# Another order of the memory places in three of the scan's rings

## The chip, the cores and the metric

The kernel runs on one core of one Trainium2 chip. The metric is the device time of one execution in microseconds; three runs are shown for the kernel before.

## The reference, cut to what matters

The program is a two-layer backbone over 256 context tokens and 1024 latent tokens, width 1024, 16 heads of 64. What bears on this change is the first layer: an RWKV mixer, which projects its tokens, runs a recurrent scan in two directions over the result and reads it out.

```python
k = xk @ lp['wk']
v = xv @ lp['wv']
def step(s, inp):
    w_t, k_t, v_t, a_t, b_t = inp[:5]
    sa = jnp.einsum('bhvk,bhk->bhv', s, a_t)
    s = s * w_t[:, :, None, :] + sa[..., None] * b_t[:, :, None, :] + v_t[..., None] * k_t[:, :, None, :]
    y = jnp.einsum('bhvk,bhk->bhv', s, inp[5])
    return s, y
s_fin, ys = lax.scan(step, s0, xs, reverse=reverse)
out = (yn + bonus) * st['g']
return out @ lp['wo']
```

Behind the mixer come a squared-ReLU MLP, a Fourier mixer and a second MLP.

## The kernel before, in words

The kernel runs through stages on one core: projections ("phase 1", 0 to about 632 us of the profile), the scan (to about 1226 us), the readout (to 1396 us), the first MLP, the Fourier mixer and the second MLP.

Phase 1 works through eight units, in the order r0, k0, r1, k1, v0, k2, v2, v1: one of the three big projections (r, k, v) over one of three column ranges (0 and 1 are the latent halves, 2 is the context). Their matmuls are on lines L621 (512 columns of tokens) and L624 (shorter forms). Beside each unit runs a low-rank part: L735 and L774 for decay and learning rate, with evictions on L793 and elementwise work on L800 to L809, and beside v1 the gate's low-rank part, whose second matmul is L578; its moving operand is a mixed token tile written by ACT (L431) and DVE (L463), and its result is evicted by L427 and L586. What the scan needs (R and a in `s_ar`, K and b in `s_bk`, v in `s_v`, the gate in `s_hg`) goes to DRAM scratch by DMAs of line L424 on SP's queue.

The scan takes 20 chunks of 64 tokens, four of them context, in two directions d = 0, 1 per step. A step loads its operands (L922, on SP's queue): a and R into a pair of tiles of ring L0/L1, K and b into ring bk, v into ring sv. Then come the scores: L957 on PE, evictions on DVE (L973, with the mask tile) and ACT (L966, L970); a triangular inverse that starts with the DVE transpose of line L1077; L1014 and L1023 bring v and the inverse into it; then the chain of states.

The readout turns y round (L1369, PE transposes), normalizes by head (DVE lines L1314 to L1328), adds and gates (L1389, L1391), splits the tile into a rounded part (L427) and the rest (L1276), and multiplies by wo: three matmuls (L368, L369, L370) for each product, "main matmuls" below. L1415 adds the result to the residual stream; L1442, L1447, L1449 and L1453 make the RMS norm of the MLP behind it, and L1472 and L1477 apply it. The 192 main matmuls of the last token range run from 1372 us to 1396 us.

On-chip memory is divided into places (U0 to U31, and X, S, W, M). Three tables name which rings lie in which places: FIRST_RINGS (tiles named a..), P1_RINGS (b..) and SCAN_RINGS (s..). A name such as sU_199 is a tile of the scan in a U place: sU_201 and 200 are U0 and U1, 199 and 198 are U2 and U3, 195 and 194 are U6 and U7, 189 is U12; bW_105 and sW_153 are both place W6, and bW_109 is W2. `slot(name)` hands out a ring's entries in turn. Two lines of `memory` make a ring entry of a later stage wait for all users that the same place had before:

```python
plan.follows.setdefault(k, []).extend(self.taken.get(p, ()))
self.taken[p] = self.taken.get(p, []) + keys
```

In phase 1 the places U2 and U3 hold moving tiles (ring x_) and U12 and U13 weights (ring w), both used to phase 1's last unit; U6 and U7 hold the context's tokens (ring hc), used by the context units k2 and v2; U14 holds latent tokens (hl). Place W6 is the last entry of ring pre, from which v1's results are stored, and later holds the scan's mask tile, loaded on L848.

A planner (class Plan) takes all operations with their dependences and costs. It starts the operation with the earliest planned start next, and among equals the one with the longest remaining tail, picks a PSUM bank or an engine where there is a choice, and so writes one program in order for each engine. PE also gets filler matmuls (L1851) where the plan sees it wait for a bank. On the chip every engine runs its program strictly in that order.

Of the kernel before, what the change touches and what calls it, by code (L numbers as in the profile page):

```python
# [18 lines left out]
P = 128  # L19
# [7 lines left out]
C = 64  # L27
# [53 lines left out]
class Plan:  # L81
# [194 lines left out]
_u = lambda *n: tuple((f"U{j}", 0) for j in n)  # L276
_halves = lambda *n: tuple((f"U{j}", at) for j in n for at in (0, 512))
SCAN_RINGS = (
    ("bk", (8, P), *_row(4, "X0", 0, 1024)), ("mab", (2, 16, 32), *_row(3, "X1", 0, 1024)), ("tr", (16, 32), ("X1", 3072)), ("vt", (8, 32), ("X1", 3584)),
    *[(f"L{h}", (8, P), *[(f"U{2 * j + h}", 0) for j in range(6)]) for h in range(2)],  # L280
    ("sv", (2, 8, C), *_u(12, 13, 14)), ("l2", (8, 2, C), *_u(15, 16, 17, 18, 19, 20)), ("bkt", (2, 8, C), *_u(21, 22, 23, 24, 25)),
    ("xd", (16, 32), ("U26", 0)), ("xt", (16, 32), ("U26", 512)), ("hp", (16, 32), ("U27", 0)), ("z", (16, 2, 16), ("U27", 512)),
    ("xs", (512,), ("S6", 0), ("W5", 0), ("W4", 0)), ("t", (8, C), ("U30", 0), ("U30", 512)), ("st", (8, C), ("U31", 0), ("U31", 512)),
    ("ta", (512,), ("S0", 0), ("S1", 0)), ("td", (16, 32), ("S2", 0), ("S3", 0)), ("x", (16, 16), ("S4", 0), ("S4", 256)),
# [1678 lines left out]
```

## Time and profile before

| | |
|---|---|
| median of three runs | 3021.74 us (3017.54 to 3023.11) |
| profiled execution, its own time | 3018.24 us |
| span of the profiled execution | 3016.5 us |
| mean granted clock of TensorE | 0.947 |
| PE busy | 2820.9 us (94%) |
| DVE busy | 1883.4 us (62%) |
| ACT busy | 997.1 us (33%) |

PE is TensorE's matmuls, DVE VectorE, ACT ScalarE, POOL GpSimd and SP the engine that issues most DMAs. "Busy" is a mean over all stages, which differ: a stage in which PE is full is bound by PE, and one in which no engine is full is bound by waits from one engine to another.

### The profile page before, as it was taken

The numbers are of one execution on the slowest core, as the hardware profiler recorded it, in microseconds if no ns is written. First come the engines' busy times: TensorE is split into PE (matmuls) and PEld (weight loads), VectorE is DVE, ScalarE is ACT, GpSimd is POOL, SyncE is SP. The second block draws the span as 40 slices with busy tenths as digits, with TensorE's granted clock in tenths as the row PEclk, the third lists the DMA queues.
The fourth block names the chain that finished last, engine by engine and source line by source line (L and its number), as shares of the span: only waits on it lengthen the run. The fifth ranks groups of instructions, "written<-read, shape, count | busy, mean of one in ns | idle before, by whom it ended". The sixth has DMA issues, their size and how long they took to land.

```text
span 3016.5 us, 63005 instructions
## 1 busy us (share of the span) xinstructions
PE 2820.9 (94%) x26640; PEld 2187.5 (73%) x26640; DVE 1883.4 (62%) x3380; ACT 997.1 (33%) x1971; POOL 496.4 (16%) x425
## 2 busy tenths in 40 slices
PE   9999989988878878899999999999899999999998
PEld 5443446467777767788788888887797888888887
DVE  5398685537777777787565565446876454454455
ACT  4264454445555655342212111212332111111111
POOL 2064353300000000120101011101421011011110
PEclk9999989978888888899999999999799999999999
DMA  9266475633444454622332232111211111111111
GB/s 283 84 167 187 133 194 169 183 98 100 131 137 135 139 151 131 216 95 84 99 108 88 87 109 91 53 57 34 86 40 48 49 57 47 38 56 50 39 42 57
DMA packets 297291, 312.88 MB, mean 104 GB/s; under 512 B 81024, under 2 KB 212224, under 8 KB 297008
## 3 DMA queue, kind: packets, MB, share of 16 engines
q1 hardware_dynamic: 295648, 304.01, 33.5%
q0 software_dynamic: 1360, 4.84, 0.5%
q8 instruction: 209, 3.42, 0.5%
q14 instruction: 74, 0.61, 0.1%
HBM read 246.38 MB, written 62.39 MB: 102 GB/s over the span
## 4 chain that ended last, share of the span: by engine, by line
PE 70%; DVE 11%; issue 4%; DMA 3%; ACT 3%; POOL 0%; SPq 0%; DVEq 0%; ACTq 0%; POOLq 0%
PE ps L368 17%; PE ps L370 17%; PE ps L369 17%; PE ps L621 4%; PE ps L624 3%; PE ps L957 2%; PE ps L1037 1%; PE ps L1059 1%; PE ps L1023 1%; DVE bU L460 1%; PE ps L1160 1%; PE ps L1014 1%; DVE rU L1276 1%; PE ps L1147 1%; DVE bS L803 1%
## 5 line engine op out<-in xcount | busy, mean ns | idle before, releaser
L368 PE MATMUL ps<-rU,rU 128*128 128x512 f32 (+3 forms) x2632 | 979.9, 372 | 13.6 <-DVE rX L1546 8.0
L370 PE MATMUL ps<-rU,rU 128*128 128x512 f32 (+3 forms) x2632 | 976.5, 371 | 8.0 <-DVE rU L1276 5.3
L369 PE MATMUL ps<-rU,rU 128*128 128x512 f32 (+3 forms) x2632 | 975.4, 371 | 0.1
L368 PEld LDWEIGHTS ps<-rU,rU 128*128 128x128 f32 x2632 | 501.9, 191 | 107.5 <-DVE rX L1546 8.8
L370 PEld LDWEIGHTS ps<-rU,rU 128*128 128x128 f32 x2632 | 501.9, 191 | 99.8 <-DVE rU L1276 6.9
L369 PEld LDWEIGHTS ps<-rU,rU 128*128 128x128 f32 x2632 | 502.3, 191 | 90.1 <-DVE rU L1360 0.4
L1546 DVE SCALAR_TENSOR_TENSOR rX<-ps,mods,rX 128x512 f32<-128x512 f32 (+1 forms) x528 | 375.8, 730 | 123.6 <-PE ps L370 121.7
L1525 ACT ACTIVATE rS<-ps 128x512 f32<-128x512 f32 x122 | 73.1, 599 | 679.2 <-PE ps L370 678.5
L1276 POOL TENSOR_TENSOR rU<-rW,rU 128x512 fp32r<-128x512 f32 x74 | 118.7, 1609 | 1004.2 <-PE ps L370 519.1
L624 PE MATMUL ps<-bU,bU 128*128 128x512 f32 (+1 forms) x544 | 238.5, 575 | 1.2 <-ACT bX L427 0.9
L427 ACT CAST rU<-rW 128x512 fp32r<-128x512 f32 x161 | 97.2, 616 | 351.9 <-PE ps L370 255.6
L427 DVE CAST rU<-rW 128x512 fp32r<-128x512 f32 x115 | 55.2, 490 | 215.9 <-PE ps L369 210.0
L1276 DVE TENSOR_TENSOR rU<-rW,rU 128x512 fp32r<-128x512 f32 x200 | 173.2, 884 | 24.0 <-ACT rU L427 23.6
L427 DVE CAST rU<-rS 128x512 fp32r<-128x512 f32 (+1 forms) x97 | 45.0, 469 | 226.2 <-ACT rS L1528 198.9
L624 PEld LDWEIGHTS ps<-bU,bU 128*128 128x128 f32 x544 | 100.5, 193 | 107.5 <-issue 98.0
L621 PE MATMUL ps<-bU,bU 128*128 128x512 f32 x304 | 142.3, 609 | 0.0
L957 PE MATMUL ps<-sU,sX 64*128 64x128 f32 (+1 forms) x1280 | 121.9, 337 | 18.4 <-DVE sU L973 5.7
L957 PEld LDWEIGHTS ps<-sU,sX 64*128 64x128 f32 x1280 | 108.3, 240 | 28.0 <-issue 8.2
L427 ACT COPY sU<-ps 32x512 f32<-32x512 f32 (+2 forms) x186 | 96.0, 517 | 75.6 <-PE ps L1160 33.0
L1276 POOL TENSOR_TENSOR rU<-rS,rU 128x512 fp32r<-128x512 f32 x42 | 65.4, 1559 | 294.4 <-ACT rU L427 133.7
L621 PEld LDWEIGHTS ps<-bU,bU 128*128 128x128 f32 x304 | 56.5, 192 | 61.2 <-issue 57.6
L973 DVE TENSOR_TENSOR sU<-ps,sW 64x256 f32<-64x256 f32 x160 | 67.5, 422 | 50.1 <-ACT sX L966 20.4
(275 smaller groups left out, 3693.0 us busy)
## 6 DMA issues: line engine op xcount, KB each, us to landing
rW<-in_mlp_w_dram SPq DMA_DIRECT2D x256, 256.0 KB
rW<-in_k_mwt_dram SPq DMA_DIRECT2D x96, 256.0 KB
sX<-s_bk SPq DMA_DIRECT2D x40, 512.0 KB
s_ar<-bU SPq DMA_DIRECT2D x32, 512.0 KB
sU<-s_ar SPq DMA_DIRECT2D x64, 256.0 KB
sW<-in_k_mwt_dram SPq DMA_DIRECT2D x64, 256.0 KB
bU<-in_rk_wk_dram SPq DMA_DIRECT2D x48, 256.0 KB
bU<-in_rk_wv_dram SPq DMA_DIRECT2D x48, 256.0 KB
```

The lines of the kernel that those rows point to most:

```text
L368: nc.tensor.matmul(out, w[0], x[0], start=start, stop=False)
L369: nc.tensor.matmul(out, w[0], x[1], start=False, stop=False)
L370: nc.tensor.matmul(out, w[1], x[0], start=False, stop=stop)
L427: self.nc.scalar.copy(out, src) if e == "act" else self.engines[e].tensor_copy(out, src)
L460: return self.plan.flex(durs, lambda e: self.engines[e].tensor_tensor(out, a, b, op), r, w)
L621: fn = lambda B=B, x=x, w=w, ms=ms, kt=kt: nc.tensor.matmul(B.tile, x[:, ms], w, start=kt == 0, stop=kt == KT - 1)
L624: fn = lambda B=B, x=x, w=w, ms=ms, kt=kt, n=n: nc.tensor.matmul(B.tile[:, :n], w[:, ms], x[:, :n], start=kt == 0, stop=kt == KT - 1)
L957: nc.tensor.matmul(BB[hh].tile[:, j * P : j * P + nr], bk[HR[hh], q, :], L[hh][HR[hh], q, :nr], start=True, stop=True)
L973: plan.add("dve", 0.41, lambda bv=bv, ro=ro, hh=hh, q4=q4, d=d, L=L: nc.vector.tensor_tensor(L[hh][ro, q4, 0:C], bv()[ro, :, 0:C], self.ma ...
L1276: plan.flex({"dve": n / 960 + 0.07, "pool": n / 440 + 0.08}, lambda e: self.engines[e].tensor_tensor(out(1), src(), f32(out(0)), ALU.subtr ...
L1525: plan.flex({"act": 0.53, "dve": 0.6}, lambda e, B=B, s=s: nc.scalar.activation(s.tile[:, :512], B.tile, AF.Relu) if e == "act" else nc.ve ...
L1546: plan.add("dve", n / 960 + 0.12, lambda B=B, m=m, n=n, xs=xs: nc.vector.scalar_tensor_tensor(xs(), B.tile[:, :n], self.mod(layer, 5, m), ...
```

## The change

The rings of the scan keep their places and their sizes. Only the order in which they are handed out is another: for a and R the pairs of places U0/1, 2/3, 4/5, 6/7, 8/9, 10/11 become U0/1, 6/7, 8/9, 10/11, 2/3, 4/5; for v U12, 13, 14 becomes U14, 12, 13; and for the transposed b and K (ring bkt) U21 to U25 becomes U23, 24, 25, 21, 22. The waits for a place's earlier users move with the place. (The change's title names moving tiles too; they are the earlier users of U2 and U3, and P1_RINGS is untouched.)

```diff
-    *[(f"L{h}", (8, P), *[(f"U{2 * j + h}", 0) for j in range(6)]) for h in range(2)],
-    ("sv", (2, 8, C), *_u(12, 13, 14)), ("l2", (8, 2, C), *_u(15, 16, 17, 18, 19, 20)), ("bkt", (2, 8, C), *_u(21, 22, 23, 24, 25)),
+    *[(f"L{h}", (8, P), *[(f"U{2 * j + h}", 0) for j in (0, 3, 4, 5, 1, 2)]) for h in range(2)],
+    ("sv", (2, 8, C), *_u(14, 12, 13)), ("l2", (8, 2, C), *_u(15, 16, 17, 18, 19, 20)), ("bkt", (2, 8, C), *_u(23, 24, 25, 21, 22)),
```

The planner works with other waits, and so writes other programs. PE's first 571 rows (to about 497 us) are the same, and so are its last 7333 (from the last main matmuls of the readout on, 1372 us), apart from buffer numbers; what lies between is in another order. Three places are shown.

PE at the end of phase 1, before, around the last L774, which is the low-rank matmul of unit k2 (bU_, bS_ and bW_ are tiles of phase 1, aU_98 is the gate's weight, ps_ PSUM banks):

```order
L621 MATMUL ps_92<-bU_137,bU_148 128x512
L621 MATMUL ps_90<-bU_137,bU_148 128x512
L774 MATMUL ps_94<-bU_129,bS_116 128x256
L774 MATMUL ps_95<-bU_129,bS_116 128x256
L774 MATMUL ps_97<-bU_129,bS_115 128x256
L774 MATMUL ps_96<-bU_129,bS_115 128x256
L735 MATMUL ps_94<-bF_206,bF_204 128x256
L578 MATMUL ps_95<-bW_109,aU_98 128x512
L578 MATMUL ps_94<-bW_105,aU_98 128x512
L578 MATMUL ps_95<-bS_114,aU_98 128x512
L578 MATMUL ps_94<-bS_113,aU_98 128x512
L578 MATMUL ps_95<-bW_111,aU_98 128x512
```

The same place in the program of the change:

```order
L774 MATMUL ps_97<-bU_129,bS_116 128x256
L774 MATMUL ps_96<-bU_129,bS_116 128x256
L578 MATMUL ps_94<-bS_114,aU_98 128x512
L578 MATMUL ps_95<-bS_113,aU_98 128x512
L621 MATMUL ps_93<-bU_123,bU_131 128x512
L735 MATMUL ps_97<-bF_206,bF_204 128x256
L621 MATMUL ps_92<-bU_123,bU_131 128x512
L621 MATMUL ps_90<-bU_123,bU_131 128x512
L621 MATMUL ps_91<-bU_138,bU_130 128x512
L578 MATMUL ps_94<-bW_111,aU_98 128x512
L578 MATMUL ps_95<-bW_110,aU_98 128x512
L621 MATMUL ps_93<-bU_138,bU_130 128x512
```

Before, the four last L774 are rows 698 to 701 of PE's program, and fifteen L578 follow in one block (rows 703 to 717). In the change the last L774 is row 685, and eight of the L578 stand in pairs between L621; a block of seven is left at rows 711 to 717. Both programs then go on with L621 at row 718.

SP's queue at the handover to the scan, before (s_v<-bW_105 stores the last result of v1 from place W6; sU_199 and 198 are the a and R tiles of step 0, direction 1; sW_153 is the mask in place W6):

```order
L424 DMA s_hg<-bW_111 128x512
L424 DMA s_v<-bW_111 256x1x256
L922 DMA sU_199<-s_ar_213 64x8x64
L922 DMA sU_198<-s_ar_213 64x8x64
L424 DMA s_v<-bW_105 256x1x256
L922 DMA sU_189<-s_v 64x512 x2
L848 DMA sW_153<-in_k_mask_dram 128x512
```

And in the change, where step 0, direction 1 has its tiles in sU_195 and 194, loaded earlier in the queue:

```order
L424 DMA s_v<-bW_105 256x1x256
L848 DMA sW_153<-in_k_mask_dram 128x512
L424 DMA s_v<-bW_110 256x1x256
L424 DMA s_v<-bS_114 256x1x256
L424 DMA s_hg<-bW_111 128x512
L424 DMA s_v<-bW_111 256x1x256
L922 DMA sU_199<-s_ar_210 64x8x64
L922 DMA sU_198<-s_ar_210 64x8x64
L922 DMA sU_189<-s_v 64x512 x2
L424 DMA s_v<-bW_109 256x1x256
```

The mask's load moved from behind the last store of v1 to behind one of the earlier ones: v1's result in place W6 is now finished before those in W2 and W0. On PE, eight of step 0's 64-column score matmuls (L957, rows of the program) stood among v1's last L621 before; now sixteen do, and the sixteen of direction 1 follow directly.

PE near the end of the readout, before (rU, rS are tiles of the readout, ones_79 and spot_80 constants of the norm): the last L1442 and what follows it.

```order
L1442 MATMUL ps5_94<-rS5_13071,ones_79 32x128 x4
L1442 MATMUL ps5_94<-rS3_13046,ones_79 32x128 x4
L368 MATMUL ps7_96<-rU14_13912,rU28_13291 128x256
L369 MATMUL ps7_96<-rU14_13912,rU28_13291 128x256
L370 MATMUL ps7_96<-rU14_13912,rU28_13291 128x256
```

In the change (L1851 is a filler):

```order
L370 MATMUL ps4_93<-rU17_13748,rU29_13431 128x256
L1442 MATMUL ps2_91<-rS0_13030,ones_79 32x128 x4
L1442 MATMUL ps2_91<-rS6_13201,ones_79 32x128 x4
L1851 MATMUL ps1_90<-ident_63 128x128 x7
L1453 MATMUL ps1_90<-rS1_13128,spot_80 128x128 x4
L1851 MATMUL ps5_94<-ident_63 128x128 x28
L1369 MATMUL ps5_94<-ident_63,rS1_13128 128x128
```

Between the last L1442 and the last range's block of main matmuls stood 192 main matmuls before (24, 72, 24, 30, 24 and 18, with transposes between them, rows 3966 to 4190). Now 24 stand there (12 and 12), with 72 fillers, and 216 main matmuls stand in one block ahead of the last L1442 (rows 3918 to 4133). Before, there were 13 fillers at this place.

## Rows read from the trace of the kernel before

**Rows 1.** The page: the span, and busy time of three engines with its share of the span and the number of instructions.

```profile
span 3016.5 us, 63005 instructions
PE 2820.9 (94%) x26640; PEld 2187.5 (73%) x26640; DVE 1883.4 (62%) x3380; ACT 997.1 (33%) x1971; POOL 496.4 (16%) x425
```

**Rows 2.** Busy time by stretch of the span: its two ends and its length, then busy us of PE, PEld (weight loads), DVE, ACT and POOL, the granted clock of PE, the DMA share and GB/s.

```profile
497.00:580.00 83.00, 82.66 (x260) 41.45 (x261) 51.07 (x89) 37.91 (x92) 34.06 (x40) 1.00 0.65 178
580.00:600.00 20.00, 15.43 (x34) 6.04 (x31) 14.54 (x21) 7.92 (x17) 11.75 (x15) 0.83 0.70 157
630.00:640.00 10.00, 4.00 (x29) 2.73 (x28) 1.54 (x4) 1.87 (x5) 1.04 (x2) 0.79 0.44 132
640.00:670.00 30.00, 28.45 (x407) 26.52 (x408) 20.91 (x57) 18.57 (x48) 1.82 (x2) 0.50 0.30 89
700.00:1226.00 526.00, 420.71 (x14022) 386.97 (x14024) 386.61 (x954) 297.36 (x657) 13.48 (x24) 0.84 0.45 134
1226.00:1300.00 74.00, 61.53 (x587) 58.98 (x584) 61.07 (x101) 27.62 (x56) 19.52 (x15) 0.93 0.65 210
1300.00:1330.00 30.00, 28.75 (x266) 27.69 (x265) 29.96 (x52) 13.84 (x28) 5.55 (x4) 1.00 0.39 124
1330.00:1350.00 20.00, 20.00 (x191) 19.34 (x190) 12.07 (x16) 5.09 (x8) 5.63 (x4) 1.00 0.11 35
1350.00:1372.00 22.00, 19.05 (x141) 18.63 (x140) 19.47 (x34) 11.90 (x20) 5.48 (x4) 0.84 0.32 102
1372.00:1396.00 24.00, 24.00 (x207) 24.00 (x206) 13.05 (x32) 2.62 (x5) 0.00 (x0) 1.00 0.45 143
```

**Rows 3.** PE in order of time at the end of phase 1 and the start of the scan: start, length of the row (of all its instructions together), line, count, and in brackets how long PE had been idle before it and who ended that.

```profile
565.38 14.00 PE L621 MATMUL ps<-bU,bU 128*128 128x512 f32 x32
579.31 1.13 PE L774 MATMUL ps<-bU,bS 64*128 64x256 f32 x8
...
582.75 1.88 PE L578 MATMUL ps<-bS,aU 128*128 128x512 f32 x4
...
587.37 2.12 PE L578 MATMUL ps<-bW,aU 128*128 128x512 f32 x4 [1.02 <-DVE bW L463]
592.92 3.78 PE L578 MATMUL ps<-bS,aU 128*128 128x512 f32 x4 [3.42 <-DVE bS L463]
596.49 4.48 PE L578 MATMUL ps<-bW,aU 128*128 128x512 f32 x8
...
625.11 6.28 PE L621 MATMUL ps<-bU,bU 128*128 128x512 f32 x14
...
638.85 4.12 PE L957 MATMUL ps<-sU,sX 64*128 64x64 f32 x32 [5.69 <-DVE sU L973]
```

**Rows 4.** DVE in order of time, with the same columns: the first step of k2's last elementwise work, the first masked eviction of the scan, and the first transpose of the inverse.

```profile
580.55 0.30 DVE L800 TENSOR_SCALAR bS<-bS 128x256 f32<-128x256 f32 x1 [8.02 <-ACT bS L793]
...
638.37 1.78 DVE L973 TENSOR_TENSOR sU<-ps,sW 64x256 f32<-64x256 f32 x4 [13.50 <-DMA sW<-in_k_mask_dram]
...
644.22 1.04 DVE L1077 STREAM_TRANSPOSE sS<-sX 128x512 f32<-128x512 f32 x1 [0.34 <-ACT sX L970]
```

**Rows 5.** SP's queue in order of time: start of issue, its length, and the DMA.

```profile
572.01 1.92 SPq L424 DMA_DIRECT2D s_bk<-bU  x3
...
585.04 2.14 SPq L424 DMA_DIRECT2D s_bk<-bU  x3
...
590.42 1.93 SPq L424 DMA_DIRECT2D s_bk<-bU  x3
...
632.75 0.58 SPq L424 DMA_DIRECT2D s_v<-bW  x1
633.38 1.25 SPq L922 DMA_DIRECT2D sU<-s_v  x2
635.43 0.34 SPq L848 DMA_DIRECT2D sW<-in_k_mask_dram  x1
```

**Rows 6.** PE in order of time in the readout: a long row of fillers, the last L1442, the L1453 behind it, the last transposes and fillers, and the first main matmul of the last range.

```profile
1249.00 8.65 PE L1851 MATMUL ps<-ident 128*128 128x128 f32 x76
...
1336.86 0.64 PE L1442 MATMUL ps<-rS,ones 128*32 128x128 f32 x16
...
1366.35 2.35 PE L1369 MATMUL ps<-ident,rS 128*128 128x128 f32 x20
...
1370.65 3.06 PE L1851 MATMUL ps<-ident 128*128 128x128 f32 x26
1373.47 0.37 PE L368 MATMUL ps<-rU,rU 128*128 128x256 f32 x1
```

**Rows 7.** DVE in order of time over the same stretch, from the norm's reciprocal to the splits that the last range's matmuls read.

```profile
1338.03 0.95 DVE L1449 RECIPROCAL rS<-rS 128x128 f32<-128x128 f32 x1 [0.58 <-ACT rS L1447]
1340.58 0.48 DVE L1415 SCALAR_TENSOR_TENSOR rX<-ps,mods,rX 128x256 f32<-128x256 f32 x1 [1.60 <-PE ps L370]
1342.16 2.27 DVE L1472 SCALAR_TENSOR_TENSOR rS<-rX,gs,rS 128x512 f32<-128x512 f32 x3 [1.10 <-ACT rS L427]
...
1366.55 0.48 DVE L1415 SCALAR_TENSOR_TENSOR rX<-ps,mods,rX 128x256 f32<-128x256 f32 x1 [2.53 <-PE ps L370]
...
1371.75 1.89 DVE L1276 TENSOR_TENSOR rU<-rS,rU 128x512 fp32r<-128x512 f32 x3
```

## Prediction

> **What bounds the kernel now.** I read the page's totals first: PE is busy for 94% of the span [rows 1], so on the whole time is saved only where PE waits or runs slowly. The table by stretch says where that is. PE is full to 580 us, has holes from 580 to 600 and from 630 to 640, runs at a granted clock of 0.50 from 640 to 670, and is 80% busy in the scan (420.71 of 526), where DVE is 73% busy: there no engine is full, and waits from one engine to another set the pace [rows 2]. So a scan that starts earlier should end earlier by about as much. In the readout DVE is full from 1300 to 1330 and PE from 1330 to 1350; from 1372 PE is full [rows 2]. As all programs are the same from 1372 us on, the question is when PE gets to that point.
>
> Then I read PE in order of time. Behind the 32 L621 come the last L774 at 579.31; the L578 that follow wait 1.02 and 3.42 us for DVE's line L463 [rows 3]. DVE itself had stood idle for 8.02 us before 580.55, because the L774 came so late [rows 4]: k2's elementwise work then stands ahead of the L463 that the L578 need. At the scan's start PE waits 5.69 us before 638.85 [rows 3], for a bank that DVE's L973 has to empty. That L973 had waited for the mask [rows 4], and SP issues the mask's load at 635.43, last in a row of stores and loads that reaches back to 632.75 [rows 5].
>
> **The change part by part.** It adds and removes no arithmetic; loads, stores and products are the same. Work moves in three places.
>
> *1. The gate's low-rank block.* In the change the last L774 is ahead of sixteen L621 that it stood behind; 32 take 14.00 [rows 3], so it comes 7 us earlier, and somewhat more as k2's second half no longer alternates with v0. The L578 are spread, and the last seven come at about the same place as before. The waits of 1.02 and 3.42 us should go: 4.4 us. Behind them twelve L578 took 3.78 + 4.48 = 8.26 us, where four usually take 1.88 [rows 3], so 5.64: another 2.6 us of low clock (0.83 over the 20 us [rows 2]). Together 7.0 us. What is late next: the stores of K and b (s_bk) are single-buffered; three go out at a time, and the last triples were issued at 572.01, 585.04 and 590.42 [rows 5], 5.4 us apart when nothing else holds them. Two triples behind 572.01 at that spacing end at about 583, 7 to 8 us earlier than now, and no more than that. The L463 for the last L578 would come 7 to 8 us earlier, against a PE that is 7 us earlier: nothing is left over. Bounds of that back pressure: 0 and 3.4 (the larger wait stays); I take 1.
>
> *2. The handover.* The last L621 end at 631.4 (625.11 + 6.28 [rows 3]). The first L973 starts 7.0 us behind that, and the inverse's first transpose 12.8 us behind it, at 644.22 [rows 4]. In the change the mask is loaded behind the store of a result that is finished some twelve L621 and sixteen score rows earlier, about 6 us. From that store's issue to the mask's is now 635.43 - 632.75 = 2.7 us [rows 5], and from there to L973 2.9 us, so the mask lands at about the end of the last L621, perhaps 1 us later. Direction 1's a and R lie in U6 and U7, loaded long before, so its scores follow directly. From L973 to the transpose stay 5.85 us [rows 4]; the transpose then stands about 7 us behind the last L621, not 12.8. The gain is 5.7 us, the 5.69 that PE waits [rows 3]. Bounds: 0, if the mask's wait on SP, which now has stores of v queued behind it, holds up the evictions from W0 and W2 that free banks; 8, if all of the 12.8 but the 5.0 of two score-and-eviction rounds goes.
>
> *3. The clock after the handover.* From 640 to 670 PE is busy for 28.45 of 30 us at a granted clock of 0.50, half of its 2.4 GHz, after a stretch in which it was busy for 4.00 of 10 [rows 2]. With the wait gone the clock may stay up. DVE is busy for 20.91 us in those 30 and its work doesn't shrink, so the bounds are 0 and 9; I take 1.5, near 0, because the scan afterwards has room on PE (80%) and does not go faster for it [rows 2].
>
> The Trainium skill ("TensorE: Matmul & The Clock Gate", section "What's actually happening") says that the half rate is the default and that recent activity lifts it. The trace agrees as far as the fall goes: 4.00 of 10 us busy, then 0.50. By that rule alone all of the 30 us would run at the full clock, and the sum would be some 7 us lower than mine.
>
> *4. The end of the readout.* This speaks against the change. Before, the last L1442 of the norm is at 1336.86, and from there to the last range's first main matmul at 1373.47, 36.6 us, PE has 192 main matmuls to do [rows 6] while DVE runs the norm and the last readout units, from 1338.03 on [rows 7]. A main matmul costs 0.116 us (207 in 24.00 [rows 2]), so the cover is 22.3 us. In the change 168 of these 192 are done ahead of the last L1442, which therefore comes 168 x 0.116 = 19.5 us later, at about 1356.4 in the old time; only 2.8 us of cover is left. How long the rest now takes has two bounds. From PE's rows alone: 32 transposes (20 take 2.35), 24 main matmuls, 1 us of L1453 and L1442, and 72 fillers (13, recorded as 26, take 3.06 [rows 6], so 72 take 16.9) make 24.5 us, and the last range starts at 1380.9: 7.4 us later. From DVE's chain: its 36.6 us hold waits for main matmuls of 1.60, 1.10 and 2.53 us [rows 7], which go; 31.4 remain, and the last range starts at 1387.8: 14.3 later. (PE's own waits there are only 2.95 us now, 22.00 - 19.05 [rows 2]; so nearly all of it is new.) DVE, full from 1300 to 1330, gets room from having to do its part later, and five fillers fewer run early in the readout, 1.2 us. I take 10, between the bounds.
>
> Sum against the profiled execution's own 3018.24: -7.0 + 1 - 5.7 - 1.5 + 10 = -3.2, so **3015 us**. That execution lies 3.5 us below the median of the runs shown (3021.74); what counts as no change is 0.2%, 6 us.
>
> **The rivals.** *A, the readout costs little.* DVE works ahead, because it no longer shares its full 1300 to 1330 with so many gating steps, and PE reaches the last L1442 earlier by most of the 12.5 us that it is idle from 1226 to 1300 (74.00 - 61.53 [rows 2]). For it: that idle time exists. Against it: the 72 fillers take PE's time whatever DVE does. Loss 0 instead of 10: 3005.
>
> *B, the clock.* All of the half-clock stretch is won back, 9 us instead of 1.5, and the readout costs its 10: 3007.5. Against it: the inverse is a chain through DVE and ACT, which were busy 20.91 and 18.57 of the 30 us [rows 2].
>
> *C, slower.* One mechanism: behind the last L1442 the chain through ACT and DVE keeps its whole 36.6 us, because each step waits for the one before and not for PE. Then the last range comes the full 19.5 us later, and the sum is -13.2 + 19.5 = +6.3: 3024.5. It decides from a loss of 19.2 on. For it: few of DVE's rows in that stretch show a wait for PE [rows 7], and 36.6 us is what the chain takes today. Against it: 5.2 us of it are such waits.
>
> *D, the change does nothing at the handover.* If v1's other stores and loads of v, and not the mask, set the scan's start, 5.7 of the gain goes, and the clock's 1.5: 3022.
>
> **How the numbers follow.** My forecast has a chance of 0.42, with its own range of 3009 to 3020; A 0.22, B 0.08, C 0.18, D 0.10. The range over all must leave out no more than 2 in 10: from below A with a little of B on top, 3000, to a little above C, 3027. Faster by over 0.2% (below 3012) are A, B and a third of my own case, 0.43; slower (above 3024) most of C and a little of D, 0.20; the rest, 0.37, is within 0.2%.
>
> **What would show it.** Right: no wait of the L578 for L463 and four of them in about 1.9 us; the first L973 within 2 us of the last L621 and the first L1077 about 7 behind it, at some 631 instead of 644; a readout in which PE stands or runs fillers for about 20 us between the last L1442 and the last range's first main matmul, which comes at about 1370. Wrong: if that matmul comes before 1362, the readout's price was mine only (A, B); if after 1376, C or D holds; if the distance from the first L1077 to the readout's first transposes differs by over 4 us, a reordered scan has a price of its own, which this sum sets at nothing because both programs run the same steps with neither PE nor DVE full.

## The result, and the profile after

The changed kernel takes 3030.85 us (median of six runs, 3026.94 to 3041.48) against 3019.64 us for the kernel before in the same comparison: a ratio of 1.0047, 95% interval 1.0032 to 1.0062. It is slower by some 14 us (10 to 19); 3015 was predicted, in a range of 3000 to 3027. The profiled execution has a span of 3028.9 us, 12.4 us more than before [rows 1].

The start of the scan came as forecast and better. PE in order of time at the end of phase 1, in the change (columns as in [rows 3]):

```profile
565.23 0.70 PE L774 MATMUL ps<-bU,bS 64*128 64x256 f32 x4
...
587.08 1.88 PE L578 MATMUL ps<-bS,aU 128*128 128x512 f32 x4
588.79 3.60 PE L578 MATMUL ps<-bW,aU 128*128 128x512 f32 x8
...
622.06 1.98 PE L621 MATMUL ps<-bU,bU 128*128 128x512 f32 x4
623.98 2.00 PE L957 MATMUL ps<-sU,sX 64*128 64x64 f32 x32
```

No L578 waits any more, and twelve of them take 5.48 us, not 8.26. The last L621 ends at 624.04, not 631.39, and the scores of step 0 follow it without a gap. DVE and SP at the handover (as in [rows 4] and [rows 5]):

```profile
619.68 0.88 DVE L973 TENSOR_TENSOR sU<-ps,sW 64x256 f32<-64x256 f32 x2 [0.60 <-ACT sX L966]
...
628.33 1.05 DVE L1077 STREAM_TRANSPOSE sS<-sX 128x512 f32<-128x512 f32 x1 [1.02 <-ACT sX L970]
```

```profile
576.55 1.95 SPq L424 DMA_DIRECT2D s_bk<-bU  x3
...
581.21 1.98 SPq L424 DMA_DIRECT2D s_bk<-bU  x3
...
613.53 0.33 SPq L848 DMA_DIRECT2D sW<-in_k_mask_dram  x1
```

The mask's load is issued at 613.53 instead of 635.43, L973 no longer waits for it but for ACT, and the first transpose of the inverse stands at 628.33 instead of 644.22: 15.9 us won.

The scan then gives all of it back. The first L1023 of steps 0, 8, 16 and 19 (the matmuls that bring inverse and right side together) show its two ends and two places between, before:

```profile
683.84 1.97 PE L1023 MATMUL ps<-sS,sU 64*64 64x64 f32 x32
...
903.63 0.33 PE L1023 MATMUL ps<-sW,sU 64*64 64x64 f32 x2
...
1135.06 0.33 PE L1023 MATMUL ps<-sW,sU 64*64 64x64 f32 x2
...
1220.03 0.33 PE L1023 MATMUL ps<-sW,sU 64*64 64x64 f32 x2 [0.46 <-ACT sU L427]
```

and in the change:

```profile
668.33 1.97 PE L1023 MATMUL ps<-sS,sU 64*64 64x64 f32 x32
...
879.60 0.30 PE L1023 MATMUL ps<-sW,sU 64*64 64x64 f32 x2 [0.69 <-DVE sU L427]
...
1138.68 0.33 PE L1023 MATMUL ps<-sW,sU 64*64 64x64 f32 x2 [0.46 <-ACT sU L427]
...
1220.75 0.33 PE L1023 MATMUL ps<-sW,sU 64*64 64x64 f32 x2 [0.23 <-ACT sU L427]
```

From the first to the last are 536.2 us before and 552.4 in the change, "scan length" below. The lead is 15.5 us at step 0, 24.0 at step 8, and gone at step 16: steps 8 to 16 take 259 us instead of 231, while the steps ahead of them and behind them take 8.5 and 2.9 us less than before. The granted clock over the whole scan is 0.87 in the change and 0.84 before, so the clock is not what makes it longer.

The readout's end costs what its order let expect. PE, as in [rows 6], in the change:

```profile
1356.15 0.43 PE L1442 MATMUL ps<-rS,ones 128*32 128x128 f32 x8 [0.88 <-ACT rS L1435]
1356.51 1.83 PE L1851 MATMUL ps<-ident 128*128 128x128 f32 x14
...
1359.06 6.42 PE L1851 MATMUL ps<-ident 128*128 128x128 f32 x56
...
1372.05 7.03 PE L1851 MATMUL ps<-ident 128*128 128x128 f32 x46 [1.95 <-ACT rS L1385]
...
1383.05 3.29 PE L1851 MATMUL ps<-ident 128*128 128x128 f32 x28
1386.09 0.36 PE L368 MATMUL ps<-rU,rU 128*128 128x256 f32 x1
```

The last L1442 is 19.3 us later than before, PE runs 18.6 us of fillers behind it (7 + 28 + 23 + 14 of them, recorded as twice that), and the last range starts at 1386.09, 12.6 us later than before [rows 6]. Of these, 11.9 arise behind the scan: from the first L1023 of step 19 to the last range are 165.3 us now and were 153.4. From there both programs run alike, and the spans differ by 12.4 us.

### The profile page after: what moved, and what is told of

Same layout as the page of the kernel before. It is cut to its first block, busy times and chain, and to the rows that moved or that the text cites. A ratio compares the mean times of both kernels' runs of the same rounds, so it can differ in the third digit from the quotient of the medians.

```text
span 3028.9 us, 63221 instructions
## 1 busy us (share of the span) xinstructions
PE 2816.7 (93%) x26750; PEld 2183.0 (72%) x26750; DVE 1883.3 (62%) x3377; ACT 997.9 (33%) x1978; POOL 489.9 (16%) x421
## 4 chain that ended last, share of the span: by engine, by line
PE 70%; DVE 12%; issue 4%; ACT 4%; DMA 3%; POOL 0%; SPq 0%; DVEq 0%; ACTq 0%
PE ps L368 17%; PE ps L370 17%; PE ps L369 17%; PE ps L621 4%; PE ps L624 3%; PE ps L957 2%; PE ps L1037 1%; ACT sU L427 1%; PE ps L1023 1%; DVE sU L973 1%; DMA rW<-s_y 1%; PE ps L578 1%; PE ps L1160 1%; DVE rU L1276 1%; PE ps L1059 1%
## 5 line engine op out<-in xcount | busy, mean ns | idle before, releaser
L368 PE MATMUL ps<-rU,rU 128*128 128x512 f32 (+3 forms) x2632 | 978.9, 372 | 12.2 <-DVE rX L1546 8.0
L427 DVE CAST rU<-rS 128x512 fp32r<-128x512 f32 x98 | 46.5, 480 | 230.5 <-ACT rS L1528 203.2
L621 PE MATMUL ps<-bU,bU 128*128 128x512 f32 x304 | 142.3, 606 | 0.0
L957 PE MATMUL ps<-sU,sX 64*128 64x128 f32 (+1 forms) x1280 | 116.0, 329 | 15.7 <-issue 5.2
L957 PEld LDWEIGHTS ps<-sU,sX 64*128 64x128 f32 x1280 | 103.4, 233 | 23.7 <-issue 8.7
L437 POOL TENSOR_SCALAR sU<-sS,sS 128x256 f32<-128x256 f32 x23 | 11.1, 486 | 556.9 <-DVE sS L1110 510.1
L621 PEld LDWEIGHTS ps<-bU,bU 128*128 128x128 f32 x304 | 56.0, 192 | 61.1 <-issue 58.2
```

The source lines that it names most:

```text
L368: nc.tensor.matmul(out, w[0], x[0], start=start, stop=False)
L427: self.nc.scalar.copy(out, src) if e == "act" else self.engines[e].tensor_copy(out, src)
L621: fn = lambda B=B, x=x, w=w, ms=ms, kt=kt: nc.tensor.matmul(B.tile, x[:, ms], w, start=kt == 0, stop=kt == KT - 1)
L957: nc.tensor.matmul(BB[hh].tile[:, j * P : j * P + nr], bk[HR[hh], q, :], L[hh][HR[hh], q, :nr], start=True, stop=True)
```

## Experiments

**Four mixtures of the two orders.** The planner is replaced by a list: for each operation its number, engine, place and fillers, in the order in which the planner of one or the other kernel had put it. Handover, scan and readout can then have either kernel's order. Where a place of the list isn't free in the mixture, the one that has been free longest is taken.

```diff
     def emit(self):
-        (the planner's loop over what is ready)
+        for entry in zlib.decompress(base64.b85decode(SEQUENCE)).decode().split(";"):
+            i, e, fills, slots = entry.split(",")
+            op, e, fills = real[int(i)], ENGINE_NAMES[int(e)], int(fills)
+            ...
+            for _ in range(fills if blank else 0):
+                self.fill(blank.tile)
+            op["fn"](e) if "durs" in op else op["fn"]()
```

e1 has the changed handover, and scan and readout in the old order:

> Places as changed. The order of all operations is written out instead of planned: the changed kernel's order up to the end of scan step 2, the order of the kernel before from there on, scan and readout. Theory 1 (each stretch's order has its own price: handover -16 us, scan +16, readout +12.6, as the two traces put it): about 3003, 16 us (to 24, the lead at step 3) under the kernel before. Theory 2 (something later holds the scan's end whatever its start, so any lead is lost on the way): no gain at the readout's first transposes, 3015 to 3020. Theory 3 (the places themselves cost the scan time): like theory 2.

e2 has the changed handover, the old scan and the changed readout:

> Places as changed, the changed order up to the end of scan step 2, the old order for the rest of the scan, the changed order from the scan's end on. Theory 1: -16 to -24 + 12.6, so 3 to 11 us under the kernel before. Theory 2: +12.6, like the changed kernel, near 3031. Theory 3: like theory 2.

e3 has the old handover, and scan and readout in the changed order:

> Places as before, the old order up to the end of scan step 2, then the changed kernel's order for the scan and the readout. Theory 1: +16 (to 24) + 12.6, so 3048 to 3056, the slowest of all. Theory 2: +12.6 alone, near 3031, as with the changed kernel. Theory 3: +12.6 at most, as the places are the old ones.

e4 has the old handover and scan, and the changed readout:

> Places and order as before up to the scan's end, the changed kernel's order from there on (the last range's main matmuls ahead of the norm). All three theories of the scan: +12.6 us, near 3032; the last L1442 some 19 us later than in the kernel before and the last range's first main matmul 12.6 later. If it is under +5, the readout's loss came from how the scan ended and not from its own order.

| | handover, scan, readout | median us (3017.93 for before) | ratio, 95% | scan length |
|---|---|---|---|---|
| e1 | new, old, old | 3002.71 | 0.9943 (0.9924 to 0.9962) | 537.8 |
| e2 | new, old, new | 3022.31 | 1.0013 (1.0000 to 1.0027) | 533.7 |
| e3 | old, new, new | 3050.63 | 1.0111 (1.0091 to 1.0132) | 555.9 |
| e4 | old, old, new | 3036.25 | 1.0060 (1.0043 to 1.0076) | 534.4 |

The ends of e1's and of e3's scan, as above for the two kernels:

```profile
667.25 1.97 PE L1023 MATMUL ps<-sS,sU 64*64 64x64 f32 x32
...
1205.03 0.32 PE L1023 MATMUL ps<-sW,sU 64*64 64x64 f32 x2 [0.46 <-ACT sU L427]
```

```profile
683.85 1.97 PE L1023 MATMUL ps<-sS,sU 64*64 64x64 f32 x32
...
1239.77 0.33 PE L1023 MATMUL ps<-sW,sU 64*64 64x64 f32 x2
```

Started early or late, in old or new places, the old order of the scan takes 534 to 538 us and the changed one 552 to 556. So theories 2 and 3 fall: a scan that starts 16.6 us earlier does end 15.0 us earlier, if its own order stays (e1), and the new places cost nothing that can be seen in it. By ratio the handover is worth -17 us (e1; -23 to -11), the readout +18 (e4; 13 to 23), and the scan's order +15 (e3 less e4; some 8 either way). The sum, +16, is near the changed kernel's +14, and handover and readout together (e2, +4) miss theirs by 3; e2 had been expected under the kernel before. e1 is faster than both kernels.

How the loss divides between scan and readout is less sure than its sum, because the readout's price hangs on the scan in front of it. The last range's first main matmul in e3 and in e4:

```profile
1405.82 0.36 PE L368 MATMUL ps<-rU,rU 128*128 128x256 f32 x1
```

```profile
1393.08 0.36 PE L368 MATMUL ps<-rU,rU 128*128 128x256 f32 x1
```

From the first L1023 of step 19 to there are 166.0 us in e3, nearly the changed kernel's 165.3, but 172.1 in e4 and 178.9 in e2, whose scans have the old order; with the old readout it is 153.4 before and 150.9 in e1. So the changed readout costs 12 to 13 us behind the scan that it was planned with, and 18.7 and 25.5 behind the other (e2's profiled execution lies 6 us above its median). e4's 18 is that of a mixture and not the price in the changed kernel, and e3 less e4 makes the scan's part too small: by the scan lengths it is 16.2 in the change and 19.7 in e3.

**The two parts of the change, planned as ever.** e9 turns only the ring of a and R, e10 only those of v and of bkt:

```diff
-    *[... for j in range(6)]) for h in range(2)],
+    *[... for j in (0, 3, 4, 5, 1, 2)]) for h in range(2)],
```

> One part of the change alone, planned as ever: only the ring of a and R takes its places in the new order. SP's queue has the mask early, as in the changed kernel; the readout has the old order (192 main matmuls between the last L1442 and the last range, 13 fillers). Theory 1 (each stretch's order has its own price): handover -16 us and no readout loss; with a scan as long as the old one about 3003, with one as long as the changed one about 3019. The handover itself must show the first L1077 near 628.

```diff
-    ("sv", (2, 8, C), *_u(12, 13, 14)), ... ("bkt", (2, 8, C), *_u(21, 22, 23, 24, 25)),
+    ("sv", (2, 8, C), *_u(14, 12, 13)), ... ("bkt", (2, 8, C), *_u(23, 24, 25, 21, 22)),
```

> The other part alone: the rings of v and of the transposed b and K in the new order, a and R as before. Handover and readout stand in the old order on all engines but a few SP rows. All theories: within 0.2% of the kernel before, near 3018.

e9 takes 3006.81 us against 3015.15, a ratio of 0.9977 (0.9957 to 0.9996), in a comparison in which both kernels spread widely (2997 to 3018, and 3008 to 3031). That is 7 us (1 to 13), where some 15 had been expected with a scan as long as the old one. Its profile has the early handover (first L1077 at 629.93), a scan of 539.4 us and the old readout; the last range starts at 1358.93, 14.5 us earlier than before:

```profile
1356.11 3.06 PE L1851 MATMUL ps<-ident 128*128 128x128 f32 x26
1358.93 0.37 PE L368 MATMUL ps<-rU,rU 128*128 128x256 f32 x1
```

The order of its scan is neither the old nor the changed one, so 539.4 prices a third order.

e10 takes 3021.36, a ratio of 1.0022 (1.0011 to 1.0033), with the first L1077 at 647.08 and a scan of 539.1. That is 7 us slower than the kernel before, just over the 0.2% that was expected at most, though all engines but SP have the rows of the kernel before in the same order and SP has all but two; why is open. The new places of these two rings may cost a little, or a difference of this size comes from elsewhere.

So the early start comes with the ring of a and R, and neither part alone has the changed kernel's scan or readout. The rings of a and R and of v together, built but not run, give the changed kernel's order row for row on all engines: the ring bkt has no part in the order, and the two losses need the other two rings turned together.

**What in the changed order makes the scan long.** Its side work differs: between the L1023 of steps 8 and 16, the changed order puts 40 of the 64 products that make the modulation vectors (DVE, L898; 64 weight tiles of 256 KB, L897), the old order 27. Twelve kernels cut or double parts of that side work, or free it of a wait, with the order of all engines untouched. All but e13 and e14 get a wrong modulation by it.

```diff
-        self.plan.add("q", 0.8, lambda: nc.sync.dma_start(w(), src), ...)
+        z = 8 if isinstance(kw, tuple) and kw in self.full else 512; self.full.add(kw)
+        self.plan.add("q", 0.8, lambda: nc.sync.dma_start(w()[:, :z], src[:, :z]), ...)
```

> The kernel before, order untouched; of the 64 weight tiles that the scan loads on the side for the modulation vectors (line L897, 256 KB each) all but the first four loads are cut to 8 of 512 columns, so the modulation is wrong and 15 MB are not moved. Read beside the same cut in the changed kernel: scan length from the first L1023 of step 0 to the first of step 19, 536.2 us before and 552.4 us in the change, a difference of 16.2. Theory A (PE's instruction supply waits behind data loads, and the changed order bunches loads): both scans get shorter, the changed one by 10 us or more beyond this one, and PE's waits with no visible cause (60 us here, 78 in the change) fall in both. Theories B and C: both shorter by a like amount, the difference stays at 12 to 18.

> The changed kernel with the same cut of side loads. Theory A: scan 552.4 falls to under 535, the difference to the old order under 6 us. Theory B (the side products on DVE, L898, of which the changed order has 40 between steps 8 and 16 and the old one 27, hold DVE): difference stays at 12 to 18. Theory C (the interleave of the scan's own operations): stays too.

e7 and e8 cut the products too:

```diff
-            w(), w(), 1.0, self.silr, ALU.mult, ALU.mult,
+            w()[:, :n], w()[:, :n], 1.0, self.silr[:, :n], ALU.mult, ALU.mult,
```

> The kernel before with the side loads cut as above and the 64 side products on DVE (L898) cut from 512 to 8 columns, order untouched; the modulation is wrong. Theory B: the scan gets shorter, and the difference to the changed order with the same cut falls under 6 us. Theory C: difference 12 to 18.

> The changed kernel with the side loads and the side products cut. Theory B: its scan falls by 10 us more than that of the kernel before with the same cut. Theory C: the difference of 12 to 18 us is still there, so it lies in the order of the scan's own operations.

e11 and e12 leave the loads whole and let the products read a constant tile:

```diff
-            w(), w(), 1.0, self.silr, ALU.mult, ALU.mult,
+            self.silr, self.silr, 1.0, self.silr, ALU.mult, ALU.max,
```

> The changed kernel, order untouched and all side loads whole, but the scan's 64 side products on DVE (L898) read a constant tile instead of the loaded one, so DVE never waits for a load; the modulation is wrong. If the loads cost the scan time by holding DVE in its queue, the scan (552.4 us from the first L1023 to the last step's) falls to about 535, as with the loads cut. If it is the loads' traffic, which delays other transfers and what PE has to fetch, it stays above 545.

> The kernel before with the same cut of the wait, as a control: no wait of a product for its load was seen in its scan, so 533 to 537 us.

e13 and e14 issue each side load twice in a row (`[nc.sync.dma_start(w(), src) for _ in range(1 + isinstance(kw, tuple))]`), e15 and e16 are e7's cut of the products with whole loads, e17 and e18 are e6 with z = 64 and z = 256:

> The kernel before, order untouched, each of the scan's 64 side loads (L897) issued twice into the same tile, so 16.8 MB more move; the result is unchanged. If traffic of the side loads costs scan time in proportion, in the old order too (3 us for cutting 15 MB), the scan of 536.2 us gets 3 to 5 longer. If an order loses only where its loads meet something, it may lose up to 20. If traffic costs nothing, 533 to 539.

> The changed kernel with each side load issued twice. Traffic theory: cutting 15 MB took 18 us off its scan of 552.4, so 16.8 MB more add 10 to 20 (562 to 572). If the loss is the interleave of the scan's own operations and the fall with the loads cut was something else: 550 to 556.

> The changed kernel with all side loads whole, and the 64 side products on DVE cut from 512 to 8 columns (the modulation is wrong). Traffic theory: the scan stays at 548 or more. If DVE's extra products in steps 8 to 16 were the cause: about 535.

> The kernel before with the same cut of the products, loads whole. Control: between 522.9 (loads and products cut) and 536.2 (nothing cut); traffic theory: about 526, so a difference of over 20 us to the changed order.

> The changed kernel with all but the first four side loads cut to 64 of 512 columns (the modulation is wrong). If the side loads' traffic is what makes the changed scan long, 534 to 539 us, as with 8 columns (534.4). If that single look was an exception and the loss lies in the interleave of the scan's own operations, 545 or more.

> The same with 256 of 512 columns. Traffic theory: between, 541 to 547. Interleave theory: 548 to 556, like the whole loads.

Scan length in us, each from one profile, and the part from step 8 to step 16:

| side work | old order | changed order | difference | steps 8 to 16: old, changed, difference |
|---|---|---|---|---|
| whole | 536.2 | 552.4 | 16.2 | 231.4, 259.1, 27.7 |
| loads of 256 columns | | 541.2 (e18) | | 247.5 in the change |
| loads of 64 columns | | 541.2 (e17) | | 249.8 in the change |
| loads of 8 columns | 533.2 (e5) | 534.4 (e6) | 1.2 | 233.3, 248.7, 15.4 |
| loads twice | 621.2 (e13) | 639.2 (e14) | 18.0 | 269.0, 313.4, 44.4 |
| products short, loads whole | 531.8 (e16) | 543.9 (e15) | 12.1 | 233.6, 252.9, 19.3 |
| products and loads short | 522.9 (e7) | 534.7 (e8) | 11.8 | 230.0, 243.3, 13.3 |
| products don't wait for loads | 547.2 (e12) | 557.5 (e11) | 10.3 | 238.6, 261.7, 23.1 |

The old order's five uncut scans (the kernel before, e1, e2, e4, e10) lie between 533.7 and 539.1, so a single look is good to some 3 us. Four things follow.

The products' waits for their loads are not the cause: freed of them, the changed scan is not shorter (e11). The control missed its expectation by 10 and is longer as well, for a reason that stays open.

The doubled loads don't measure traffic. Both loads of a pair write one tile, and on SP's queue the second waits for the first; the queue's waits in e13's and in e14's scan (us in total, times, longest):

```profile
SPq L897 <- DMA sW<-in_k_mwt_dram: 286.2, 64, 9.2
```

```profile
SPq L897 <- DMA sW<-in_k_mwt_dram: 268.3, 64, 9.0
```

The scan's other loads stand behind these in the queue. Both orders lose alike, 85.0 and 86.8 us, where 3 to 5 (at most 20) and 10 to 20 had been expected, and the rate only rises from 132 to 141 and from 130 to 138 GB/s. So e13 and e14 show what a held queue costs.

The side work is a part of the changed order's loss. In steps 8 to 16, where that loss lies, cutting the loads takes 9 to 12 us off the changed scan (e6, e17, e18), cutting the products 6 (e15) and cutting both 16 (e8); the old one gains next to nothing there (231.4 whole, 230.0 to 233.6 cut). The loads' size matters little: e18 and e17 are alike though one moves four times the other's bytes, and e17 fell between the two lengths expected for it, as e15 did.

But it isn't all. With loads and products cut the changed order is still 11.8 us longer, and 13.3 in steps 8 to 16. The 1.2 of e5 and e6, which theory A asked for, doesn't fit that: e6 has the shortest steps 0 to 8 and 16 to 19 of all changed scans, and with one look at each it is open whether that is chance. What is left can only lie in how the scan's own operations are interleaved, by e7 and e8 some 12 of the 16 us; no run here takes it apart further.

One thing in which the two orders differ there can be read from the trace: PE's longest waits for nothing that the profile names. Busy time by stretch, in the change (columns as in [rows 2]):

```profile
859.00:864.30 5.30, 4.57 (x222) 4.08 (x218) 5.09 (x17) 3.50 (x8) 0.00 (x0) 1.00 1.04 231
864.30:869.40 5.10, 0.02 (x4) 0.02 (x4) 0.00 (x0) 1.22 (x2) 0.00 (x0) 0.82 1.02 244
...
931.30:936.50 5.20, 0.04 (x6) 0.01 (x2) 1.95 (x7) 0.00 (x0) 0.00 (x0) 0.61 0.88 229
```

PE stands for 5.1 us in the middle of a run of equal matmuls, and the profile shows no engine or transfer that it waits for ("issue"):

```profile
930.93 0.40 PE L1160 MATMUL ps<-sU,sU 32*32 32x32 f32 x25 [0.47 <-DVE sU L1152]
...
936.49 1.60 PE L1160 MATMUL ps<-sU,sU 32*32 32x32 f32 x103 [5.16 <-issue]
```

The trace has the transfers of kind "instruction" too, in this window one of 16 KB on queue q8 (packets, MB, share of the 16 engines):

```profile
q8 instruction: 1, 0.02, 1.3%
```

It lasts from 934.00 to 935.09, 1.4 us before PE goes on; in the wait that ends at 869.38 another ends at 867.90, 1.5 us before. Such transfers come some 130 times in the scan, every 4 us or so, and all 21 "issue" waits of PE over 1.5 us in the change, and all 15 in the kernel before, end 1.3 to 1.7 us after one of them does. So by their timing PE waits there for its instructions. The side loads don't make these waits: with loads and products cut, in e8, the same one stands behind the same 25 matmuls, with the transfer engines 0.61 busy:

```profile
924.38 0.40 PE L1160 MATMUL ps<-sU,sU 32*32 32x32 f32 x25
930.44 1.60 PE L1160 MATMUL ps<-sU,sU 32*32 32x32 f32 x103 [5.66 <-issue]
```

All "issue" waits in the scan come to 60 us before and 80 in the change; in steps 8 to 16 they are 24 and 39, and 24 and 35 with the side work cut (e7, e8). That is a good part of what the two orders differ by, but waits that overlap others don't add up to a price: e1 has 75 in a scan as short as the old one, 33 of them in steps 8 to 16, which take 234 us. What they cost was not tried by itself.

## Why the prediction was wrong

**The gate's block.** Right: -7.0 was forecast, v1's last L621 end 7.35 us earlier, with eight more score rows ahead of it. The back pressure, taken at 1, did not show: the last two triples of s_bk went out at 576.55 and 581.21, 8.5 and 9.2 us earlier than before, and no L578 waited.

**The handover.** Right in mechanism, small by some 3 us: -5.7 was forecast for the mask; from the last L621's end to the first transpose are 4.3 us now and were 12.8, so 8.5, over the upper bound of 8. What was mis-sized is when the mask comes: it was expected at about the end of the last L621, and its load is issued 10.5 us before that end, so that the first L973 start at 619.68, inside v1's tail.

**The clock.** 1.5 was forecast, and the rival gave 9; nothing of either shows. From the first L1077 to the first L1023 are 40.0 us now and were 39.6, and the granted clock from 640 to 670 is 0.50 in the change too, though PE had been busy for 7.33 of the 10 us ahead and is busy for 27.99 of the 30:

```profile
630.00:640.00 10.00, 7.33 (x113) 6.12 (x110) 8.18 (x25) 7.95 (x22) 0.00 (x0) 0.77 0.46 122
640.00:670.00 30.00, 27.99 (x583) 26.21 (x585) 24.54 (x61) 18.12 (x48) 0.96 (x2) 0.50 0.20 68
```

So the Trainium skill's sentence that recent activity lifts the half rate ("TensorE: Matmul & The Clock Gate", section "What's actually happening") does not agree with this stretch if the profile's busy share is taken for activity; the measurement decides against rival B.

**The scan.** This is the step that failed: "a scan that starts earlier should end earlier by about as much", with the scan's reordering set at nothing "because both programs run the same steps with neither PE nor DVE full". The first half holds (e1: 537.8 us, started 16.6 us earlier). The second does not: the order of the same steps, which the change rewrote throughout, is by itself worth 16.2 us in the change and 19.7 in e3, where neither the start nor the places are new. Why that order is slower is shown in part only: some of it is side work bunched in steps 8 to 16, the rest the interleave of the scan's own operations. A sum of what moved at three places could not see it; the diff of the programs shows rows of the scan moved throughout, and the 40 against 27 side products could have been counted in it beforehand. The prediction had named the sign: a distance from the first L1077 to the readout's first transposes that differs by over 4 us. Those transposes, before and in the change:

```profile
1226.56 0.33 PE L1369 MATMUL ps<-ident,rS 128*128 128x128 f32 x1
```

```profile
1224.53 0.66 PE L1369 MATMUL ps<-ident,rS 128*128 128x128 f32 x4
```

The distance was 582.3 us and is 596.2, 13.9 more.

**The readout.** Right in mechanism and size: +10 was forecast between bounds of 7.4 and 14.3, and 11.9 is measured behind the scan. The last L1442 was put at 1356.4 in the old time and stands at 1356.15, as the scan, its lead lost, ends at about the old time. From there to the last range are 29.9 us, between the 24.5 by PE's rows and the 31.4 by DVE's chain.

**The rivals.** Without the scan the measured terms are -7.4 - 8.5 + 11.9 = -4.0, near the forecast -3.2; the scan's 16.2 bring them to 12.2, and the spans differ by 12.4. So the one term set at nothing made the sign. Rival C had the sign but not the place, and its 3024.5 is 6 us short: the chain behind the last L1442 took 29.9 us and not its whole 36.6. The last range's first main matmul comes at 1386.09, behind the 1376 from which "C or D holds", and neither does, for D's loss at the handover did not come either. A case of a scan with a price of its own was not among the rivals.

## What to carry to other kernels

A change of memory places in a planned kernel is a change of the whole order behind it: price the stretches whose rows move even where every row is still there, above all those in which no engine is full. Write the order out as data and mix the stretches of two orders: here that found, in four runs, the part worth 17 us and the two that ate it, and one mixture is faster than both kernels. Read each stretch of a mixture beside the same stretch in its own kernel, too: behind a scan that it was not planned with, the readout cost 19 us and more instead of 12. And try the parts of a change one by one: the ring of a and R alone keeps the early start and the old readout.

## What was not expected of the hardware

PE stood for up to 5.2 us inside a run of equal 32x32 matmuls. All 36 of its waits over 1.5 us for which the profile names no cause, in the two kernels' scans, end 1.3 to 1.7 us after a 16 KB transfer of instructions does. And it ran at half its clock from 640 to 670 while busy for 93% of the time.
